# Full-row decay and rate products in preparation, attention's low parts on VectorE, and a later place for the first early operands

## The chip, the core and the metric

The kernel runs on one core of one Trainium2 chip. The metric is the device time of one execution in microseconds (us); the time before is the median of three executions. A profile is of one execution.

Engine names as in the profile: PE is TensorE (PEld its weight loads), DVE is VectorE, ACT is ScalarE, POOL is GpSimd, SP is SyncE, whose queue issues nearly all transfers between device memory and SBUF. "L514" is line 514 of the kernel.

## The reference

One layer of a hybrid encoder on 1024 tokens of width 1024, all in float32:

```
u = rmsnorm(h); cols = u @ w_in              # RWKV-7, HGRN2 and gate columns
rwkv7:  cols = cols + mu * (token_shift(cols) - cols)
        r, k, v, w_lo, a_lo, g_lo = split(cols)          # w_lo and a_lo: 64 columns each
        w_log = -softplus(-(w0 + tanh(w_lo) @ w2)) - 0.5  # decay
        a     = sigmoid(a0 + a_lo @ a2)                   # rate
        ... generalised delta-rule state over time, group norm, bonus, output gate
hgrn2:  ... gated linear recurrence in chunks of 64
h = h + (gate_a * y_a + gate_b * y_b) @ w_out
q, k, v = (rmsnorm(h) @ wq), (rmsnorm(mem) @ wk), (rmsnorm(mem) @ wv)   # 4 heads of 256, 256 memory tokens
h = h + softmax(q k / 16) v @ wo
h = h + (silu(u @ w1) * (u @ w3)) @ w2       # u = rmsnorm(h)
out = rmsnorm(h)
```

## The kernel before

**Products in three parts.** TensorE multiplies in a rounded float32 form. To keep the accuracy, an operand x is split: the high part is x rounded (a copy, on ACT, L282), the low part is x minus the high part (a subtraction, L286, on POOL or on DVE as `lo_eng` says). A product is then three matmuls into one PSUM tile (`mm3`, L300 to L302): high x high, high x low, low x high, 128 rows by 128 columns of weights against 512 or 256 columns. In the profile whi, wh, ah are high parts and wlo, wl, al low parts; whT and wlT are the parts of the first early operands of the feed-forward block.

**Stages.** Preparation (`rw_prep`, up to about 400 us) takes the RWKV columns in eight column blocks j of 128 and two halves h of 512 tokens: projections (pproj, 24 matmuls each) shifted in time, and between them `factors(j, h)`, which makes the decay sg and the rate aa from the low-rank columns. These lie in two tiles lw and la: of lw rows 0 to 63 hold the high part of tanh(w_lo) and rows 64 to 127 its low part; la the same for a_lo, with the halves exchanged. `LR` lists for each its tile, the rows of the high part (`own`) and those of the low part (`other`). The weight w2h holds the high part of w2 (or a2) twice, in both halves of the rows, so one matmul over 128 rows adds high x high and low x high. The third part, the low part of the weight (w2l) against the high part of the column, is a matmul over the 64 rows `own` alone (L514). Both write the PSUM tile pza. `tile_inputs(j)` makes w2h and w2l (L482, POOL); their pool has two buffers.

Mixing (to about 1298 us) has an order written out by the kernel's own planner; the change does not touch it. Then comes `attention_block`: values and keys (pvv, pk) from `mem`, the split of the mixed output y (`yraw`), the output product with w_out (`add_project`, PSUM tile pw), queries, scores, softmax and attended values for both token halves, and `add_project` with wo for each half. Beside the two kinds of output product run `w2_sums` (sums and differences of blocks of ffn_w2, stored for later) and, in the second half with wo, `early_blocks`: transposes (L1813), high and low parts (L1816 to L1819, L1820) of the feed-forward input of the first token half. Its PSUM tiles and those of the output product share eight buffers.

After it the feed-forward block works on half-size blocks with fewer products (seven for eight). Its first operands are made early: `weights(f, True)` loads the weights for f = 0 and 1, and `early_operands` makes from them differences on DVE (L2078, L2081, L2082) and splits them (whT, wlT; ACT and POOL) for the first products P5 and P4. The raw weights have ten buffers.

**What sets the order.** Outside mixing, a list scheduler fills each engine's queue: of the instructions that its simulation finds ready it takes the one earliest in the program; `high_priority(n)` counts a block's instructions as n places earlier. The queues then run in that order on the chip, each waiting for its own first instruction. The loads of the early weights are ordered on SP behind the last loads of wo (`behind`).

Of the kernel before, what the change touches and what calls it, by code (L numbers as in the profile page):

```python
# [18 lines left out]
P = 128  # L19
# [165 lines left out]
def tile_trunk(ctx, tc, x, mem, norm_mix_g, w_in, rw_mu, rw_w0, rw_w2, rw_a0, rw_a2, rw_g2,  # L185
# [93 lines left out]
    def split(hi, lo, src, hi_eng="act", lo_eng="pool"):  # L279

        if hi_eng == "act":
            nc.scalar.activation(hi, src, AF.Copy)  # L282
        else:
            nc.vector.tensor_copy(hi, src)
        e = nc.gpsimd if lo_eng == "pool" else nc.vector
        e.tensor_tensor(lo, src, hi.bitcast(F32), op=ALU.subtract)  # L286
# [136 lines left out]
    def rw_prep(rctx):  # L423
# [49 lines left out]
        def tile_inputs(j):  # L473
            w2r = fp.tile([P, 2, P], F32, tag="w2r", name="w2r", bufs=1)
            for n, w2 in enumerate((rw_w2, rw_a2)):
                for b in (0, 64):
                    nc.sync.dma_start(out=w2r[b:b + 64, n, :], in_=w2[0, :, j * P:(j + 1) * P])
            w2h = fp.tile([P, 2, P], F32R, tag="w2h", name="w2h")
            w2l = fp.tile([P, P], F32R, tag="w2l", name="w2l")
            nc.scalar.activation(w2h, w2r, AF.Copy)  # L480
            for n, (_, own, _) in enumerate(LR):
                nc.gpsimd.tensor_tensor(w2l[own, :], w2r[own, n, :], w2h[own, n, :].bitcast(F32), op=ALU.subtract)  # L482
            carry = fp.tile([P, 3], F32, tag="carry", name="carry")
            lnb = fp.tile([P, P], F32, tag="lnb", name="lnb")
            nc.sync.dma_start(out=lnb, in_=rw_ln_b[0, j * P:(j + 1) * P].partition_broadcast(P))
            krv = [[fp.tile([P, HALF], F32, tag=n, name=n, bufs=4) for h in range(NHALF)] for n in "krv"]
            tiles[j] = krv, w2h, w2l, lnb
            for n, mui in enumerate((8 + j, j, 16 + j)):
                if j == n == 0:
                    ahead.append(load_w(cols.pop(0)))  # L490
                    yield
                w = ahead.pop(0) if j == n == 0 else column()
                for h in range(NHALF):
                    if h and j == n == 0:
                        ahead.append(load_w(cols.pop(0)))
                    shifted(krv[n][h], w, mui, h, carry[:, n:n + 1])
                    yield
# [3 lines left out]
        def factors(j, h):  # L501
# [6 lines left out]

            sg, aa = T("sg"), T("aa")
            for n, (dst, bias) in enumerate(((sg, "w0"), (aa, "a0"))):  # L510
                t, own, _ = LR[n]
                ps = pz.tile([P, HALF], F32, tag="z", name="pza")
                nc.tensor.matmul(ps, w2h[:, n, :], t[:, sl], start=True, stop=False)
                nc.tensor.matmul(ps, w2l[own, :], t[own, sl], start=False, stop=True)  # L514
                nc.scalar.activation(dst, ps, AF.Sigmoid, bias=vc(bias, j))
            cum = T("cum")
            nc.vector.tensor_tensor_scan(cum, rst64, sg, 0.0, op0=ALU.mult, op1=ALU.add)
# [1130 lines left out]
    def attention_block(xctx):  # L1648
# [16 lines left out]
                nc.sync.dma_start(out=raw, in_=s3[:, k:k + 2, :])  # L1665
                yield k, raw

        def load_w(src, col, lo_eng=None):

            w = []  # L1670
            for k, raw in load_raw(src, col):
                hi, lo = (wp.tile([P, 2, W], F32R, tag=n, name=n) for n in ("whi", "wlo"))
                split(hi, lo, raw, lo_eng=lo_eng or ("pool", "dve")[k // 2 % 2])
                w += [(hi[:, n, :], lo[:, n, :]) for n in range(2)]
            return w

# [10 lines left out]
        def values(c):  # L1687
            cs = slice(c * HALF, (c + 1) * HALF)
            ps = [pp.tile([P, HALF], F32, tag="p", name="pvv") for _ in range(NMT)]
            for k in range(KT):  # L1690
                raw = w0.pop(0) if w0 else value_raw(c, k)
                hi, lo = (wp.tile([P, HALF], F32R, tag=n, name=n) for n in ("whi", "wlo"))
                split(hi, lo, raw, lo_eng=("pool", "dve")[k % 2])
                for t in range(NMT):
                    mm3(ps[t], *(m[:, k // 4, k % 4, t * P:(t + 1) * P] for m in mT), hi, lo, k == 0, k == KT - 1)
            for t in range(NMT):
                nc.scalar.activation(Vh[:, t, cs], ps[t], AF.Copy)
                nc.vector.tensor_tensor(Vl[:, t, cs], ps[t], Vh[:, t, cs].bitcast(F32), op=ALU.subtract)
# [23 lines left out]
        def w2_sums(fs, steps):  # L1722


            def load(f, y):
                for r in range(2):
                    rows = slice((f + r * HF) * P, (f + r * HF + 1) * P)
                    nc.sync.dma_start(out=y[:, 2 * r:2 * r + 2, :].rearrange("p c t -> p (c t)"), in_=ffn_w2[0, rows, :])

            def sums(f, y):  # L1730
                y11, y12, y21, y22 = (y[:, n, :] for n in range(4))
                nc.vector.tensor_tensor(y11, y12, y11, op=ALU.subtract)
                nc.gpsimd.tensor_tensor(y12, y22, y12, op=ALU.subtract)
                nc.gpsimd.tensor_tensor(y22, y22, y11, op=ALU.subtract)
                nc.vector.tensor_tensor(y21, y22, y21, op=ALU.subtract)
                nc.sync.dma_start(out=wsd[f], in_=y)

            loaded = []
            for loads, summed in steps:
                for place in loads:  # L1740
                    y, f = place(), next(fs)
                    load(f, y)
                    loaded.append((f, y))
                for _ in range(summed):
                    sums(*loaded.pop(0))
                yield
# [8 lines left out]
        def add_project(a, w, src, halves, ss=None, beside=iter(()), dst=None, between=lambda hs: None):  # L1755
# [15 lines left out]
            def split_next():  # L1771
                ck = todo[len(ww)]
                ww[ck] = [wp.tile([P, HALF], F32R, tag=n, name=n) for n in ("whi", "wlo")]
                split(*ww[ck], raws[len(ww) - 1], lo_eng=("pool", "dve")[ck[1] % 2])

            for c in range(NHALF):
                cs = slice(c * HALF, (c + 1) * HALF)
# [27 lines left out]
        def early_blocks(hs, hi, lo):  # L1805

            b12s, s1s = (vp.tile([P, HK, HALF], F32, tag=t, name="sums") for t in ("Vh", "Vl"))
            for k in range(HK):
                pts = []
                for kk in (k, k + HK):  # L1810
                    pts.append(pp.tile([P, HALF], F32, tag="p", name="pt"))
                    for i in range(4):
                        nc.tensor.transpose(pts[-1][:, i * P:(i + 1) * P], hs[i][:, kk * P:(kk + 1) * P], ident)  # L1813
                b12, s1 = b12s[:, k, :], s1s[:, k, :]
                h, l, g = hi[:, k, :], lo[:, k, :], vc("ffn", k + HK)
                nc.scalar.activation(b12, pts[0], AF.Copy, scale=vc("ffn", k))  # L1816
                nc.scalar.activation(h, pts[1], AF.Copy, scale=g)
                nc.vector.scalar_tensor_tensor(s1, pts[1], g, b12, op0=ALU.mult, op1=ALU.add)
                nc.vector.scalar_tensor_tensor(l, pts[1], g, h.bitcast(F32), op0=ALU.mult, op1=ALU.subtract)  # L1819
                split(hi[:, k + HK, :], lo[:, k + HK, :], s1)  # L1820
                nc.sync.dma_start(out=early_d[0, k], in_=b12)
                nc.sync.dma_start(out=early_d[1, k], in_=s1)
                yield
# [3 lines left out]
        for h, a in enumerate(yT):  # L1827
            for k in range(KT):
                raw = hp.tile([P, HALF], F32, tag="h", name="yraw")
                nc.sync.dma_start(out=raw, in_=yd[k, h])  # L1830
                split(a[0][:, k, :], a[1][:, k, :], raw, lo_eng="pool" if k % 2 else "dve")

        w2f = iter(range(HF))
        pairs = {}
# [230 lines left out]
    def weights(f, early=False):  # L2065

        if not early:
            return [[raw(w, k, (f + e) * P, HK, P) for e in (0, HF) for k in (0, HK)] for w in WS]
        A = [{}, {}]
        for b in (0, 2, 3, 1):  # L2070
            for n, w in enumerate(WS):
                A[n][b] = raw(w, b % 2 * HK, (f + b // 2 * HF) * P, HK, P, order=loads[min(f, 1)])
        return [[a[b] for b in range(4)] for a in A]

    def early_operands(A):
        T1, T4 = [], []
        for a11, a12, a21, a22 in A:
            tt(a21, a21, a11, op=ALU.subtract)  # L2078
            T1.append(operand(a21, "T1"))
        for a11, a12, a21, a22 in A:  # L2080
            tt(a22, a21, a22, op=ALU.subtract)  # L2081
            tt(a12, a22, a12, op=ALU.add)  # L2082
            T4.append(operand(a12, "T4"))
        return T1, T4
# [52 lines left out]

    with tc.high_priority(300):
        early = [weights(f, True) for f in range(2)]
        early = [early_operands(A) for A in early]  # L2140
    late = late_blocks()
    next(late)

    n = 0
# [181 lines left out]
```

## Time and profile before

| | |
|---|---|
| median of three executions | 2332.89 us (2332.19 to 2334.03) |
| the profiled execution | 2333.25 us, its span 2331.5 us |
| busy: PE, PEld | 2287.6 us (98%), 1863.8 us (80%) |
| busy: DVE, ACT, POOL | 1529.4 us (66%), 1136.0 us (49%), 1156.5 us (50%) |
| TensorE clock granted over the span | 0.995 |

Busy time of PE, DVE and POOL by stage, from the profile's stretches:

| stretch | us | PE | DVE | POOL | granted clock | DMA share |
|---|---|---|---|---|---|---|
| start, 0 to 100 | 100 | 84.05 | 64.10 | 43.26 | 0.97 | 0.49 |
| preparation, 100 to 380 | 280 | 280.00 | 223.70 | 141.28 | 1.00 | 0.45 |
| its end, 380 to 460 | 80 | 76.65 | 38.22 | 51.15 | 0.98 | 0.48 |
| mixing, 460 to 1298 | 838 | 832.34 | 581.89 | 488.06 | 1.00 | 0.38 |
| attention, 1298 to 1690 | 392 | 380.63 | 208.17 | 140.20 | 0.98 to 1.00 | 0.28 to 0.89 |
| feed-forward, 1690 to the end | 641.5 | 633.92 | 413.33 | 292.58 | 1.00 | 0.45 |

A row is read so: PE's busy time is the union of its matmuls' times, and a matmul counts as busy while it waits inside the pipeline, so the distance between the starts of two matmuls tells more than its duration. A share of a whole run is an average over stages with different limits; what counts is what PE waits for in a stage.

### The profile page before, as it was taken

Reading aid. Unit: us, or ns where it says so; the run is one execution under the profiler, and the core shown is the slowest. Engines: PE = TensorE matmul, PEld = TensorE weight load, DVE = VectorE, ACT = ScalarE, POOL = GpSimd, SP = SyncE. Lnnn points to the kernel's source line nnn. Section 1 sums busy time; section 2 is a strip of 40 time slices with the busy share of each in tenths; the row PEclk is TensorE's granted clock in tenths of the full one; section 3 lists DMA queues with packets and bytes.
Section 4 is the critical chain, followed back from the end, with each engine's and each line's share of the span. In section 5 each row is a group of like instructions: output and inputs, shape, how many; then the busy total and the mean of one; then the engine's idle time right before and its main releaser. Section 6 shows DMA issues by size and latency. Waiting matters only on the chain.

```text
span 2331.5 us, 47063 instructions
## 1 busy us (share of the span) xinstructions
PE 2287.6 (98%) x18262; PEld 1863.8 (80%) x18262; DVE 1529.4 (66%) x2425; ACT 1136.0 (49%) x2259; POOL 1156.5 (50%) x1201
## 2 busy tenths in 40 slices
PE   7999999999999999999999999999999999999998
PEld 5777777777888887888788778888788888888887
DVE  5787875576877767777666454544768675656655
ACT  6545455555565655654566323543453333334433
POOL 3555545655565655666566553113466555552212
PEclk9999999999999999999999999999999999999999
DMA  5344454332344343434334797215943323248653
GB/s 173 112 133 113 117 140 138 104 99 73 91 109 119 78 118 106 137 86 111 89 91 125 262 335 279 69 55 217 297 145 119 123 94 122 86 160 301 212 168 122
DMA packets 393691, 327.94 MB, mean 141 GB/s; under 512 B 107595, under 2 KB 318653, under 8 KB 392061
## 3 DMA queue, kind: packets, MB, share of 16 engines
q1 hardware_dynamic: 391549, 319.17, 44.9%
q0 software_dynamic: 1344, 4.72, 0.5%
q8 instruction: 144, 2.36, 0.4%
q10 hardware_dynamic: 576, 1.05, 0.1%
q14 instruction: 78, 0.64, 0.1%
HBM read 228.12 MB, written 96.21 MB: 139 GB/s over the span
## 4 chain that ended last, share of the span: by engine, by line
PE 76%; DVE 3%; DMA 2%; POOL 1%; issue 1%; ACT 1%; SPq 0%; POOLq 0%; ACTq 0%; DVEq 0%
PE pproj L103 21%; PE P L301 6%; PE P L302 6%; PE P L300 6%; PE acc L301 3%; PE acc L302 3%; PE acc L300 3%; PE cm L103 2%; PE pw L302 2%; PE pw L300 2%; PE pw L301 2%; PE psA L103 2%; PE psc L103 1%; PE po L103 1%; PE pq L302 1%; PE pq L301 1%
## 5 line engine op out<-in xcount | busy, mean ns | idle before, releaser
L103 PE MATMUL pproj<-uh,whi 128*128 128x512 f32 x768 | 319.9, 417 | 1.0 <-DVE q L103 1.0
L103 PE MATMUL pproj<-uh,wlo 128*128 128x512 f32 x768 | 301.0, 392 | 2.9 <-POOL wlo L103 2.3
L103 PE MATMUL pproj<-ul,whi 128*128 128x512 f32 x768 | 301.4, 392 | 0.0
L286 POOL TENSOR_TENSOR wlo<-wraw,whi 128x512 fp32r<-128x512 f32 (+1 forms) x86 | 117.0, 1362 | 224.5 <-ACT whi L282 210.0
L286 POOL TENSOR_TENSOR wl<-wraw,wh 128x512 fp32r<-128x512 f32 x87 | 121.4, 1403 | 204.4 <-ACT wh L282 160.8
L103 POOL TENSOR_TENSOR wlo<-wraw,whi 128x512 fp32r<-128x512 f32 x96 | 129.4, 1359 | 119.2 <-ACT whi L103 111.9
L282 ACT ACTIVATE whi<-wraw 128x512 fp32r<-128x512 f32 (+1 forms) x166 | 101.0, 617 | 174.5 <-PE pw L302 65.9
L300 PE MATMUL pproj<-uh,whi 128*128 128x512 f32 (+1 forms) x432 | 180.2, 417 | 1.1 <-ACT uh L328 0.7
L302 PE MATMUL pproj<-uh,wlo 128*128 128x512 f32 (+1 forms) x432 | 170.5, 395 | 1.9 <-POOL wlo L286 1.9
L103 PEld LDWEIGHTS pproj<-uh,whi 128*128 128x128 f32 x768 | 144.4, 188 | 34.3 <-DVE q L103 2.2
L103 PEld LDWEIGHTS pproj<-ul,whi 128*128 128x128 f32 x768 | 144.4, 188 | 32.4
L301 PE MATMUL pproj<-ul,whi 128*128 128x512 f32 (+1 forms) x432 | 170.2, 394 | 0.0
L103 PEld LDWEIGHTS pproj<-uh,wlo 128*128 128x128 f32 x768 | 144.9, 189 | 28.1 <-POOL wlo L103 2.7
L286 POOL TENSOR_TENSOR wlT<-wraw,whT 128x512 fp32r<-128x512 f32 x72 | 101.4, 1418 | 70.1 <-ACT whT L282 58.8
L282 ACT ACTIVATE wh<-wraw 128x512 fp32r<-128x512 f32 x143 | 87.2, 623 | 94.5 <-PE P L301 71.4
L103 ACT ACT_TABLE_LOAD x90 | 115.5, 1283 | 13.5 <-DVE m L103 6.4
L301 PE MATMUL acc<-wl,th 128*128 128x512 f32 x308 | 119.9, 389 | 0.0
L300 PE MATMUL acc<-wh,th 128*128 128x512 f32 x308 | 119.8, 389 | 0.0
L302 PE MATMUL acc<-wh,tl 128*128 128x512 f32 x308 | 119.8, 389 | 0.0
L300 PEld LDWEIGHTS pproj<-uh,whi 128*128 128x128 f32 (+1 forms) x432 | 81.5, 189 | 26.5 <-issue 6.7
L2270 DVE TENSOR_TENSOR tl<-tl,th 128x512 fp32r<-128x512 f32 x77 | 60.4, 797 | 62.6 <-ACT th L2269 62.3
L302 PE MATMUL pw<-whi,al 128*128 128x512 f32 x256 | 100.9, 394 | 0.3 <-DVE al L286 0.3
(457 smaller groups left out, 6386.2 us busy)
## 6 DMA issues: line engine op xcount, KB each, us to landing
wraw<-in_w_in_dram SPq DMA_DIRECT2D x148, 256.0 KB
wraw<-in_ffn_w_dram SPq DMA_DIRECT2D x145, 256.0 KB
y<-in_ffn_w_dram SPq DMA_DIRECT2D x22, 512.0 KB
wsum_d<-y SPq DMA_DIRECT2D x11, 1024.0 KB
hsum_d<-s SPq DMA_DIRECT2D x44, 256.0 KB
tl<-hsum_d SPq DMA_DIRECT2D x44, 256.0 KB
wraw<-wsum_d SPq DMA_DIRECT2D x44, 256.0 KB
hid_d<-s SPq DMA_DIRECT2D x33, 256.0 KB
```

The lines of the kernel that those rows point to most:

```text
L103: r = getattr(self.engine, op)(*a, **kw)
L282: nc.scalar.activation(hi, src, AF.Copy)
L286: e.tensor_tensor(lo, src, hi.bitcast(F32), op=ALU.subtract)
L300: nc.tensor.matmul(ps, ah, bh, start=first, stop=False)
L301: nc.tensor.matmul(ps, ah, bl, start=False, stop=False)
L302: nc.tensor.matmul(ps, al, bh, start=False, stop=last)
L2270: tt(hl, hl.bitcast(F32), hh.bitcast(F32), op=ALU.subtract)
```

## The change

1. Preparation: w2l becomes two tiles side by side of 128 rows each, one for the decay and one for the rate. The half of the rows that is not `own` is filled with zeros on POOL, and the matmul goes over all 128 rows of w2l and of lw or la. So the four products of a group have one form.
2. Attention: the low parts of the weights (values, keys, queries, w_out, wo) and of y, which alternated between POOL and DVE, and those of the early blocks' sums, which were POOL's, are all made on DVE. Two of the four subtractions of `w2_sums` go from POOL to DVE.
3. The early operands for f = 0 and 1 are made under `high_priority(150)` in place of 300; their loads stay at 300.

```
@@ tile_inputs
-            w2l = fp.tile([P, P], F32R, tag="w2l", name="w2l")
+            w2l = fp.tile([P, 2, P], F32R, tag="w2l", name="w2l")
             nc.scalar.activation(w2h, w2r, AF.Copy)
-            for n, (_, own, _) in enumerate(LR):
-                nc.gpsimd.tensor_tensor(w2l[own, :], w2r[own, n, :], w2h[own, n, :].bitcast(F32), op=ALU.subtract)
+            for n, (_, own, other) in enumerate(LR):
+                nc.gpsimd.memset(w2l[other, n, :].bitcast(F32), 0.0)
+                nc.gpsimd.tensor_tensor(w2l[own, n, :], w2r[own, n, :], w2h[own, n, :].bitcast(F32), op=ALU.subtract)
@@ factors
                 nc.tensor.matmul(ps, w2h[:, n, :], t[:, sl], start=True, stop=False)
-                nc.tensor.matmul(ps, w2l[own, :], t[own, sl], start=False, stop=True)
+                nc.tensor.matmul(ps, w2l[:, n, :], t[:, sl], start=False, stop=True)
@@ load_w of attention
-                split(hi, lo, raw, lo_eng=lo_eng or ("pool", "dve")[k // 2 % 2])
+                split(hi, lo, raw, lo_eng="dve")
@@ values
-                split(hi, lo, raw, lo_eng=("pool", "dve")[k % 2])
+                split(hi, lo, raw, lo_eng="dve")
@@ w2_sums
-                nc.gpsimd.tensor_tensor(y12, y22, y12, op=ALU.subtract)
-                nc.gpsimd.tensor_tensor(y22, y22, y11, op=ALU.subtract)
+                nc.vector.tensor_tensor(y12, y22, y12, op=ALU.subtract)
+                nc.vector.tensor_tensor(y22, y22, y11, op=ALU.subtract)
@@ split_next of add_project
-                split(*ww[ck], raws[len(ww) - 1], lo_eng=("pool", "dve")[ck[1] % 2])
+                split(*ww[ck], raws[len(ww) - 1], lo_eng="dve")
@@ early_blocks
-                split(hi[:, k + HK, :], lo[:, k + HK, :], s1)
+                split(hi[:, k + HK, :], lo[:, k + HK, :], s1, lo_eng="dve")
@@ the split of y
-                split(a[0][:, k, :], a[1][:, k, :], raw, lo_eng="pool" if k % 2 else "dve")
+                split(a[0][:, k, :], a[1][:, k, :], raw, lo_eng="dve")
@@ before the feed-forward block
     with tc.high_priority(300):
         early = [weights(f, True) for f in range(2)]
+    with tc.high_priority(150):
         early = [early_operands(A) for A in early]
```

More of the change, by code (lines that the diff above doesn't have):

```diff
@@ L510, in factors @@
             for n, (dst, bias) in enumerate(((sg, "w0"), (aa, "a0"))):
-                t, own, _ = LR[n]
+                t = LR[n][0]
                 ps = pz.tile([P, HALF], F32, tag="z", name="pza")
                 nc.tensor.matmul(ps, w2h[:, n, :], t[:, sl], start=True, stop=False)
-                nc.tensor.matmul(ps, w2l[own, :], t[own, sl], start=False, stop=True)
+                nc.tensor.matmul(ps, w2l[:, n, :], t[:, sl], start=False, stop=True)
                 nc.scalar.activation(dst, ps, AF.Sigmoid, bias=vc(bias, j))
@@ L1666, in load_raw, with load_w @@
                 yield k, raw
-        def load_w(src, col, lo_eng=None):
+        def load_w(src, col):
             w = []
```

## The prediction

> **What bounds the kernel now.** I read the page's busy times first, then busy time by stage, then what TensorE waits for, and last the order of time at the places that the change touches.
>
> ```profile
> span 2331.5 us, 47063 instructions
> PE 2287.6 (98%) x18262; PEld 1863.8 (80%) x18262; DVE 1529.4 (66%) x2425; ACT 1136.0 (49%) x2259; POOL 1156.5 (50%) x1201
> ```
>
> TensorE is busy for 98% of the span, but a matmul that waits inside its own pipeline counts as busy. So a gain can come from two places: from the idle 44 us, or from matmuls that start further apart than they need to.
>
> ```profile
> 100.00:380.00 280.00, 280.00 (x1240) 219.38 (x1239) 223.70 (x246) 136.62 (x200) 141.28 (x195) 1.00 0.45 120
> ...
> 1298.00:1440.00 142.00, 135.19 (x670) 114.10 (x669) 69.34 (x82) 47.31 (x84) 74.32 (x55) 0.98 0.89 317
> 1440.00:1600.00 160.00, 159.47 (x855) 136.44 (x854) 84.15 (x165) 80.01 (x173) 24.67 (x20) 1.00 0.28 93
> 1600.00:1690.00 90.00, 85.97 (x385) 70.28 (x384) 54.68 (x66) 35.14 (x66) 41.21 (x30) 0.98 0.88 290
> ```
>
> The columns are stretch, length, busy time of PE, PEld, DVE, ACT and POOL, granted clock, DMA share, GB/s. In preparation (100 to 380) TensorE never idles: every nanosecond between two matmul starts there is time of the kernel. In attention it idles for 142.0 - 135.2 = 6.8, 0.5 and 4.0 us, 11.4 in all. The waits of that stage say at what:
>
> ```profile
> PE pt L1813 <- DVE al L1819: 4.0, 1, 4.0
> PE pk L302 <- POOL wlo L286: 2.8, 1, 2.8
> PE pvv L301 <- POOL wlo L286: 1.7, 2, 0.9
> ```
>
> These three hold 8.5 of the 11.4 us, and all are waits for a low part on POOL or for DVE's queue, which is what the change moves.
>
> **Part A, preparation.** The order of time on PE around one group of decay and rate products (start, duration):
>
> ```profile
> 151.29 0.39 PE L513 MATMUL pza<-lw,w2h 128*128 128x512 f32 x1
> 151.61 0.49 PE L514 MATMUL pza<-lw,w2l 64*128 64x512 f32 x1
> 152.03 0.50 PE L513 MATMUL pza<-la,w2h 128*128 128x512 f32 x1
> 152.46 0.50 PE L514 MATMUL pza<-la,w2l 64*128 64x512 f32 x1
> 152.89 0.50 PE L300 MATMUL pproj<-uh,whi 128*128 128x512 f32 x1
> 153.22 0.40 PE L301 MATMUL pproj<-ul,whi 128*128 128x512 f32 x1
> 153.46 0.40 PE L302 MATMUL pproj<-uh,wlo 128*128 128x512 f32 x1
> ```
>
> Two neighbours of one form start 0.24 us apart (153.22 to 153.46). Where the form goes from 128 rows to 64 or back, the starts lie 0.32, 0.42, 0.43, 0.43 and 0.33 apart: five stretched steps, 153.22 - 151.29 = 1.93 us. With all four products on 128 rows they would be five plain steps, 5 x 0.235 = 1.18. Gain 0.75 us. Every second group stands behind transposes instead:
>
> ```profile
> 178.24 0.47 PE L513 MATMUL pza<-lw,w2h 128*128 128x512 f32 x1
> ...
> 180.26 0.40 PE L301 MATMUL pproj<-ul,whi 128*128 128x512 f32 x1
> ```
>
> Its five steps take 180.26 - 178.24 = 2.02 us. Five plain ones would take 1.18 (gain 0.84); if the first, behind the transposes, stays as long as a stretched one, 0.43 + 4 x 0.235 = 1.37 (gain 0.65). I take 0.75 here too, the middle. How often:
>
> ```profile
> L514 PE MATMUL pza<-lw,w2l x16: 492/492/502, 57.8 to 354.6; 64*128 64x512 f32 x16
> ```
>
> 16 groups x 0.75 = 12.0 us. The first two or three start before 100 us, where PE has other waits that may swallow it; I take 14 in full and two by half, 11.3 us. The cover: DVE is the next busiest, 223.7 of 280 us. Were PE to need only 280 - 13 x 0.75 = 270, DVE would stand at 83%, still not the bound, and ACT and POOL at about half. Bounds: 9 us gained (if the first and the last of the eight column blocks run into DVE) and 12.7 (8 x 0.75 + 8 x 0.84).
>
> What is added: 16 fills of a 64x128 half on POOL, in front of the subtraction in each block's input step.
>
> ```profile
> 416.83 0.21 POOL L103 MEMSET BP<- 128x128 f32 x1
> ```
>
> 16 x 0.21 = 3.4 us at most, beside 139 idle us of POOL in that stretch; the first use of the tile (57.8) comes long after it is made, so it costs nothing. The fill waits for the tile's slot, which was last read by the products two column blocks back, so it holds up nothing that is queued behind it on POOL. If POOL were full it would cost those 3.4 us.
>
> A rule that speaks against this part, with the row first:
>
> ```profile
> L300 PEld LDWEIGHTS pproj<-uh,whi 128*128 128x128 f32 x416 | 79.0, 190 | 25.5 <-issue 6.7 <-ACT uh L328 1.6 <-DVE BK L549 1.5
> ```
>
> A 128-row weight load takes 0.19 us, and yet the products start 0.24 apart with 512 columns each: the load is hidden behind the matmul before it. The Trainium skill, "TensorE: Matmul & The Clock Gate", Part 3, under what overlaps, says that a weight load overlaps with matmuls in flight only when its row group differs; by that, full-row loads would stand open and part A would bring about nothing. The trace does not bear it out for these loads.
>
> **Part B, attention's low parts, and its start.** 54 weight splits, 8 operand splits, 4 of the early blocks and 22 sums go from POOL to DVE.
>
> ```profile
> L286 POOL TENSOR_TENSOR wlo<-wraw,whi 128x512 fp32r<-128x512 f32 x54 | 74.5, 1381 | 194.9 <-ACT whi L282 180.5 <-PE pk L301 6.3 <-DMA wraw<-in_ffn_w_dram 3.8
> ```
>
> ```profile
> L286 DVE TENSOR_TENSOR wlo<-wraw,whi 128x512 fp32r<-128x512 f32 x54 | 48.7, 905 | 48.9 <-ACT whi L282 45.6 <-PE pt L322 2.0 <-DMA wraw<-in_xa_wk_dram 1.1
> ...
> L1912 DVE TENSOR_TENSOR al<-po,ah 128x512 fp32r<-128x512 f32 x16 | 11.1, 692 | 7.9 <-ACT ah L1911 7.9
> ```
>
> POOL takes 1.38 us for a weight's low part. DVE takes 0.69 for the same subtraction with one input in PSUM (last row), and 0.91 on average for the weights' low parts, whose two inputs lie in SBUF, while POOL works beside it. So 88 x 0.69 = 61 us come to DVE, and at least 54 x 0.21 = 11 of slowing go: DVE would have at most 208 + 50 = 258 of 392 us in the three stretches. It is not the bound on average; single places decide. The costliest, on PE, POOL and ACT:
>
> ```profile
> 1346.32 0.28 PE L301 MATMUL pk<-mT,whi 128*128 128x256 f32 x1
> 1349.43 0.58 PE L302 MATMUL pk<-mT,wlo 128*128 128x256 f32 x1 [2.84 <-POOL wlo L286]
> ...
> 1355.10 0.40 PE L300 MATMUL pw<-whi,ah 128*128 128x512 f32 x1
> ```
>
> ```profile
> 1347.67 1.71 POOL L286 TENSOR_TENSOR wlo<-wraw,whi 128x512 fp32r<-128x512 f32 x1
> ```
>
> ```profile
> 1343.52 1.14 ACT L282 ACTIVATE whi<-wraw 128x512 fp32r<-128x512 f32 x2
> ...
> 1352.43 0.63 ACT L282 ACTIVATE whi<-wraw 128x512 fp32r<-128x512 f32 x1 [6.82 <-DMA wraw<-in_w_out_dram]
> ```
>
> The high part is there at 1344.7 and the low part only at 1349.4, behind other low parts on POOL. ACT makes a high part in 0.57 us and DVE alone a low part in 0.69, so DVE stays close behind ACT and ends near 1346, about when PE asks. The wait (2.84) goes, and with it the slower clock behind it (0.98 granted in this stretch is 2.8 us of full speed lost; I put 1.3 of it here, the rest behind the value waits). What is late next: the first output weights, whose split waits for their load until 1352.4; that load stands in SP's queue behind the loads of yraw, which wait for slots that the same low parts free, so it comes earlier too, by 2 us or so. At the least PE starts the output product at 1352.4 + 0.63 + 0.69 = 1353.7 instead of 1355.1, a gain of 1.4; at the most the whole 4.1 and 0.9 us of the value waits (two of 0.9 at most, of which a load hides one). I take 3.2, nearer the upper end, since all that was late hangs on the low parts.
>
> **Part C, the end of attention.** The early loads keep their priority of 300; the first operands that are made of them get 150.
>
> ```profile
> 1660.76 2.80 DVE L2081 TENSOR_TENSOR wraw<-wraw 128x512 f32<-128x512 f32 x2
> 1663.49 1.75 DVE L2082 TENSOR_TENSOR wraw<-wraw 128x512 f32<-128x512 f32 x1
> 1665.16 0.74 DVE L1819 SCALAR_TENSOR_TENSOR al<-pt,VC,ah 128x512 fp32r<-128x512 f32 x1
> ```
>
> ```profile
> 1666.04 0.63 PE L1813 MATMUL pt<-ident,tok 128*128 128x128 f32 x4 [4.03 <-DVE al L1819]
> ```
>
> Three subtractions of the early operands stand in DVE's queue ahead of the low part that frees the PSUM tile, for 1665.16 - 1660.76 = 4.4 us; beside POOL two of them take 2.80. The clock granted in this stretch, 0.98 of 90 us, is 1.8 us lost, most of it behind this wait: 4.0 + 1.4 = 5.4 in all. With 150 these subtractions rank behind that low part, so the wait should mostly go. On the other side DVE gets eight low parts more in this stretch (5.5 us) and loses about as much slowing, and it is full here; the operands for the first P5 product are needed only after the last output products. I take 4.5, bounds 5.4 gained and 4 lost (one chain of subtraction, high part on ACT and POOL's 1.4 before the first product, with the slow clock).
>
> **The rest.** The 22 sums and the output and query weights: in their stretch (1440 to 1600) PE idles for 0.5 us in all. More in DVE's queue beside the softmax can cost from -0.5 to 1.4 us (two low parts); I take 0.5 lost, the middle.
>
> Sum: -11.3 - 3.2 - 4.5 + 0.5 = -18.5. The profiled execution took 2333.25 us (span 2331.5), 0.36 above the median of 2332.89. 2333.25 - 18.5 - 0.36 = 2314.4.
>
> **Rivals.** (1) The waits of attention stay or move: the order on DVE comes out with another operand in front, or PE then waits for the output weights. For it: DVE's full queue around 1660. Then A, 1.4 from B and up to 4 lost: 2333 - 11.3 - 1.4 + 0 to 4 = 2320 to 2324. (2) Preparation does not return its time. Either each full-row load stands open behind the product before it: the steps stay at 0.24 + 0.19 = 0.43, as long as now, and the time is 2333 - 7.2 = 2326. Against it are the 0.24 us steps of all other full-row products; chance 0.03. (That is the skill's rule of Part 3 above.) Or DVE takes over as the bound of preparation, against which stands its 83%; a third of A left gives 2322; chance 0.07. (3) Slower: operands with 150 free their weight slots later; SP's queue is in order, so the next loads of the feed-forward weights block the h_d stores and the hn loads behind them, and TensorE waits for the late blocks. For it: ten slots serve 24 early loads. Against it: the first late block is needed only after six products of 12 matmuls, 6 x 12 x 0.235 = 17 us. A wait of 14.5 us eats all that A and B bring, and from 19 on the kernel is slower by 0.2%. If all 16 low parts of the early operands, 16 x 1.38 = 22 us on POOL, came in front of those loads, it would be 2333 - 14.5 + 22 = 2341.
>
> **How the numbers follow.** The forecast 0.62; rival 1 0.23; rival 2 0.10 in both forms; rival 3 0.05. The forecast's own range is 2310 (12.7 + 5.0 + 5.4) to 2319. Eight in ten: 2309 to 2323. A measurement tells about 0.2%, 4.7 us, from no change: faster needs less than 2328.2, which the forecast, rival 1 and nearly all of rival 2 give: faster 0.91; same 0.05; slower 0.04.
>
> **What would show it.** A: no 64-row pza, steps of 0.24, a block of preparation 1.5 us shorter than now. B: no wait at pk, an earlier pw. C: no 4 us wait at L1813 and a granted clock of 1.00 there. Wrong would be: blocks of preparation of the old length, new waits for DVE near 1340 to 1360 or 1680 to 1700, or a wait for hn.

## The result and the profile after

| | before | changed | ratio, 95% interval |
|---|---|---|---|
| median | 2333.46 us (2332.19 to 2334.96, 4 runs) | 2309.59 us (2308.82 to 2316.52, 4 runs) | 0.9904, 0.9884 to 0.9924 |
| the profiled execution, its span | 2333.25, 2331.5 us | 2309.72, 2308.0 us | |

The kernel is 23.9 us faster; 18.5 was forecast. The time lies 0.4 us below the forecast's own range of 2310 to 2319 and at the fast edge of the eight-in-ten range of 2309 to 2323. In a later comparison the changed kernel gave 0.9900 (0.9885 to 0.9915).

The busy times on the page of the changed kernel:

```profile
PE 2270.0 (98%) x18262; PEld 1860.1 (81%) x18262; DVE 1558.0 (68%) x2513; ACT 1134.2 (49%) x2259; POOL 1037.3 (45%) x1129
```

PE is still at 98%. DVE has 88 instructions more and 28.6 us more work, POOL 119.2 us less. Where the time went is read from stretches between the same products in both traces. Those of the changed kernel (stretch, length, busy time of PE, PEld, DVE, ACT, POOL, granted clock, DMA share, GB/s):

```profile
93.12:379.15 286.03, 285.57 (x1311) 231.98 (x1310) 229.87 (x254) 146.80 (x217) 154.00 (x217) 0.99 0.48 126
...
1291.98:1334.72 42.74, 41.12 (x242) 34.93 (x240) 27.36 (x46) 24.38 (x45) 1.57 (x3) 1.00 0.97 328
...
1567.09:1663.15 96.06, 96.06 (x439) 78.29 (x437) 65.33 (x99) 40.19 (x79) 12.02 (x8) 1.00 0.88 286
1663.15:1711.38 48.23, 47.31 (x221) 38.44 (x220) 29.77 (x42) 29.20 (x52) 32.24 (x24) 1.00 0.56 182
```

Three of the same stretches in the kernel before:

```profile
95.56:393.12 297.56, 297.02 (x1311) 231.12 (x1310) 229.48 (x254) 147.28 (x217) 152.85 (x207) 0.99 0.45 121
...
1305.30:1355.10 49.80, 43.60 (x243) 37.66 (x241) 27.72 (x30) 26.59 (x48) 30.70 (x24) 0.93 0.89 296
...
1586.34:1688.09 101.75, 97.72 (x438) 79.61 (x437) 59.37 (x76) 40.40 (x79) 42.86 (x31) 0.98 0.83 278
```

All stretches side by side:

| from, to | before | changed | difference |
|---|---|---|---|
| start, third group of decay and rate products | 95.56 us | 93.12 us | -2.44 |
| third group, end of preparation's products | 297.56 (clock 0.99) | 286.03 (0.99) | -11.53 |
| to the first product of mixing | 80.22 | 80.07 | -0.15 |
| mixing, to the first pvv | 831.96 | 832.76 | +0.80 |
| first pvv, first pw | 49.80 (clock 0.93) | 42.74 (1.00) | -7.06 |
| first pw, first transposes of the softmax | 114.57 | 115.70 | +1.13 |
| to the second pw | 116.67 | 116.67 | 0.00 |
| wo, to the first P | 101.75 (clock 0.98) | 96.06 (1.00) | -5.69 |
| first P products | 46.91 | 48.23 | +1.32 |
| the rest | 596.50 | 596.62 | +0.12 |
| sum | | | -23.50 |

So there are three gains, where the three parts were made, and two places that gave 2.4 us back. What PE waited for from 1285 to 1750 us of the changed kernel:

```profile
PE pw L300 <- ACT whi L282: 0.7, 1, 0.7
PE pvv L301 <- DVE wlo L286: 0.7, 3, 0.2
PE P L300 <- ACT hB L2021: 0.6, 1, 0.6
...
PE pw L300 <- ACT ah L282: 0.4, 1, 0.4
```

The 4.0 of the transposes, the 2.8 of pk and the 1.7 of pvv for POOL are gone. The new rows are those of pw and of P; pvv now waits 0.7 us for DVE.

### The profile page after: what moved, and what is told of

It is laid out like the page before. It is cut to its first block, busy times and chain, and to the rows that moved or that the text cites. A ratio compares the mean times of both kernels' runs of the same rounds, so it can differ in the third digit from the quotient of the medians.

```text
span 2308.0 us, 47067 instructions
## 1 busy us (share of the span) xinstructions
PE 2270.0 (98%) x18262; PEld 1860.1 (81%) x18262; DVE 1558.0 (68%) x2513; ACT 1134.2 (49%) x2259; POOL 1037.3 (45%) x1129
## 4 chain that ended last, share of the span: by engine, by line
PE 73%; DVE 4%; DMA 3%; POOL 2%; issue 1%; ACT 1%; SPq 0%; POOLq 0%; ACTq 0%; DVEq 0%
PE pproj L103 21%; PE P L301 6%; PE P L302 6%; PE P L300 6%; PE acc L301 3%; PE acc L302 3%; PE acc L300 3%; PE pw L302 3%; PE pw L301 2%; PE pw L300 2%; PE cm L103 2%; PE psA L103 2%; PE psc L103 1%; PE po L103 1%; PE pq L301 1%
## 5 line engine op out<-in xcount | busy, mean ns | idle before, releaser
L277 POOL TENSOR_TENSOR ss<-ss,nhalf 128x4 f32<-128x4 f32 (+1 forms) x7 | 6.2, 881 | 323.1 <-DMA wraw<-in_xa_wo_dram 186.6
L286 DVE TENSOR_TENSOR wlo<-wraw,whi 128x512 fp32r<-128x512 f32 x134 | 93.1, 701 | 55.3 <-ACT whi L282 53.4
L300 PE MATMUL pw<-whi,ah 128*128 128x512 f32 x256 | 100.6, 393 | 1.2 <-ACT whi L282 0.7
```

The source lines that it names most:

```text
L277: nc.gpsimd.tensor_tensor(dst, tmp, nhalf[:, 0:n], op=ALU.pow)
L300: nc.tensor.matmul(ps, ah, bh, start=first, stop=False)
```

## The experiments

The differences below are of medians within one comparison, or of landmarks (starts of the same PE product) in the traces. The landmarks scatter a little: the four kernels that leave preparation as it was start its third group 0.2 to 1.6 us and its fifth 0.2 to 3.1 us sooner than the profiled execution before, keep most of that distance to the end of preparation's products, and then lose 0.3 to 1.1 us on it in mixing. Differences of that size at those places are not read as effects; the mean over the later groups is not touched by them. One part of it may belong to the change: from 57 to 66 us the granted clock is 0.81 (1.7 us lost) in five of the seven traces with a 64-row product (not in e4 and e9), and 1.00 in all seven with full rows. No run decides whether the 64-row products bring it about.

| kernel | median, us | before beside it | ratio, 95% interval |
|---|---|---|---|
| e1_prep_only | 2320.53 | 2332.93 | 0.9949, 0.9937 to 0.9962 |
| e2_low_only | 2326.89 | 2332.93 | 0.9978, 0.9969 to 0.9986 |
| e3_prio_only | 2332.53 | 2332.93 | 0.9997, 0.9988 to 1.0007 |
| e4_no_prep | 2322.18 | 2332.93 | 0.9956, 0.9943 to 0.9969 |
| e5_decay_full | 2318.28 | 2331.13 | 0.9941, 0.9929 to 0.9954 |
| e6_half_rows_together | 2316.93 | 2331.13 | 0.9938, 0.9925 to 0.9952 |
| e7_late_first | 2309.50 | 2331.13 | 0.9907, 0.9893 to 0.9920 |
| e9_prio_late_first | 2327.51 | 2331.13 | 0.9981, 0.9972 to 0.9989 |
| e8_y_alternates | 2310.67 | 2331.84 | 0.9906, 0.9892 to 0.9921 |
| e10_wout_first | 2310.89 | 2331.84 | 0.9905, 0.9890 to 0.9920 |
| e11_both | 2306.96 | 2331.84 | 0.9889, 0.9872 to 0.9905 |
| e12_changed_again | 2309.96 | 2331.84 | 0.9900, 0.9885 to 0.9915 |

### The three parts one by one

**Preparation alone** (the kernel before with the first two hunks of the change).

> The kernel before with the change's first part alone: both low products of preparation on all 128 rows, attention as before. If the steps to and from a 64-row product are what cost (0.42 us against 0.23), each of the 16 groups starts its next product some 0.8 us sooner, preparation ends 13 to 14 us sooner, and this is all kept to the end: 2319 to 2321 us by the median before of 2333.46. If preparation's gain only looks like that because attention's part covers for it (the value weights arriving later than the rows of attention then need them), attention's first waits grow by what preparation returned and the time stays at 2324 us or more. The rest of attention, with the 3.1 us wait of pk and the 4.3 us wait at the hand-over, should be where it was.

2320.53 us, 12.4 less than before. Preparation's products end 13.3 us sooner by the trace, and the kernel's end 13.8. The waits of attention are there as before:

```profile
PE pt L1814 <- DVE al L1820: 3.9, 1, 3.9
PE pk L302 <- POOL wlo L286: 2.8, 1, 2.8
```

So preparation's time is kept, and attention does not live on it: the first theory.

**Low parts alone** (the hunks of attention, `early_operands` still at 300).

> The kernel before with the second part alone: attention's low parts and sums on VectorE, the early operands at their old priority, preparation as before. If POOL's low parts were what the 3.1 us wait of pk and the waits of pvv stood on, attention is 6 to 8 us shorter up to the query stage; the 4.3 us wait at the hand-over should stay if its cause is where the early operands stand in their queues, and go if its cause is POOL's work. First case: 2326 to 2328 us; second: 2321 to 2324 us. If VectorE's own low parts are late instead, pk's wait turns into waits of pvv and pw and the time stays at 2331 to 2334 us.

2326.89 us, 6.0 less (0.22%). The 2.8 us wait of pk is gone, the hand-over's stays nearly whole, and pw waits instead, here for its weights and then 0.8 us for ah:

```profile
PE pt L1813 <- DVE al L1819: 3.7, 1, 3.7
PE pw L300 <- ACT whi L282: 1.0, 1, 1.0
```

By landmarks this kernel gains 8.1 us from the first pvv to pk's last product, and 5.3 are left at the softmax's first transposes. The hand-over is therefore not POOL's doing: with all low parts on DVE it waits 3.7 of 4.0 us.

**The priority alone.**

> The kernel before with the third part alone: the early operands behind their loads at priority 150, everything else as before. If the place in the queue is what the 4.3 us wait at the hand-over stands on, the wait goes and the time is 4 to 6 us less: 2327 to 2330 us. If it needs the low parts on VectorE too (POOL making the low half of the second operand, behind its other low parts), the wait stays or shrinks by a part only and the time is 2331 to 2334 us. The first 1650 us should be those of the kernel before.

Neither theory: the wait at the hand-over is gone (5.6 us from there to the first P), and yet the time is the same, 2332.53 against 2332.93. The first P products give 5.0 us back. PE at that place, and DVE before it:

```profile
1720.44 0.39 PE L302 MATMUL P<-hB,wl 128*128 128x512 f32 x1
1723.72 0.49 PE L300 MATMUL P<-hB,wh 128*128 128x512 f32 x1 [2.90 <-ACT hB L2019]
1724.51 0.79 PE L301 MATMUL P<-lB,wh 128*128 128x512 f32 x1 [0.29 <-DVE lB L2020]
1725.10 0.63 PE L302 MATMUL P<-hB,wl 128*128 128x512 f32 x1
1725.53 0.63 PE L300 MATMUL P<-hB,wh 128*128 128x512 f32 x1
```

```profile
1703.36 1.23 DVE L2110 TENSOR_TENSOR T<-wraw 128x512 f32<-128x512 f32 x1 [4.82 <-DMA wraw<-in_ffn_w_dram]
1704.52 0.68 DVE L2112 TENSOR_TENSOR wraw<-T,wraw 128x512 f32<-128x512 f32 x1
1705.12 1.40 DVE L2020 SCALAR_TENSOR_TENSOR lB<-pth,VC,hB 128x512 fp32r<-128x512 f32 x2
```

A sum T of `products` waits 4.82 us at the head of DVE's queue for its load. The late blocks' lB stands behind it, then their fS, whose high parts on ACT stand ahead of the next hB, for which P waits 2.90. The products after that wait start 0.43 apart instead of 0.23. In the kernel before, the same sum comes 1705.88 - 1688.09 = 17.8 us after the first P:

```profile
1705.88 1.52 DVE L2110 TENSOR_TENSOR T<-wraw 128x512 f32<-128x512 f32 x1 [3.21 <-DMA wraw<-in_ffn_w_dram]
```

In e3 it comes 1703.36 - 1681.62 = 21.7 us after it. PE reached its first P 6.5 us sooner and the load came only 2.5 us sooner: the wait at the hand-over had covered this one. In e3 SP issues that load behind those of hn and of the early blocks, where it waits for their transfers; its record there shows no wait for a free slot.

**Low parts and priority, preparation as before.**

> The changed kernel with preparation put back: attention's low parts on VectorE and the early operands behind their loads. If the parts add up, this gives what the change gives without preparation's 13 to 14 us: 2322 to 2324 us. If the three parts overlap (one cover serving two), it is either nearer to the changed kernel (2316 us or less) or nearer to the kernel before (2327 us or more). In the traces the attention start's gain is 8 us up to pk's last product and 6 us after the waits of pw that follow; I expect the same here.

2322.18 us, 10.75 less. With e1 the ratios add up: 0.51% + 0.44% = 0.95%, against 0.96% for the whole change. Parts B and C alone give 0.22% and 0.03%, together 0.44%. That is more than their sum, by about as much as the intervals allow, so I do not build on it; the trace does not decide it, since its execution (2326.39 us) was the longest of the five.

### What a 64-row product costs

> The changed kernel, but the rate's low product on its own 64 rows again, the decay's on all 128. If each step between a 128-row and a 64-row product costs 0.2 us, two of the four such steps of a group are back: the groups' starts fall behind those of the changed kernel by 0.41 us each, preparation ends 6.5 to 7 us later, and the time is 2316 to 2317 us against 2309.6. If instead it is the change of the row group between the decay's rows and the rate's that costs, one 64-row product alone costs little and the time stays at 2310 to 2312 us.

```
+                rs = slice(0, P) if n == 0 else LR[n][1]
-                nc.tensor.matmul(ps, w2l[:, n, :], t[:, sl], start=False, stop=True)
+                nc.tensor.matmul(ps, w2l[rs, n, :], t[rs, sl], start=False, stop=True)
```

A group in the changed kernel, and the same in e5 (start, duration):

```profile
146.46 0.39 PE L515 MATMUL pza<-lw,w2h 128*128 128x512 f32 x1
146.69 0.39 PE L516 MATMUL pza<-lw,w2l 128*128 128x512 f32 x1
146.92 0.40 PE L515 MATMUL pza<-la,w2h 128*128 128x512 f32 x1
147.15 0.40 PE L516 MATMUL pza<-la,w2l 128*128 128x512 f32 x1
147.39 0.39 PE L300 MATMUL pproj<-uh,whi 128*128 128x512 f32 x1
147.62 0.39 PE L301 MATMUL pproj<-ul,whi 128*128 128x512 f32 x1
```

```profile
149.42 0.39 PE L515 MATMUL pza<-lw,w2h 128*128 128x512 f32 x1
...
149.88 0.40 PE L515 MATMUL pza<-la,w2h 128*128 128x512 f32 x1
150.21 0.49 PE L517 MATMUL pza<-la,w2l 64*128 64x512 f32 x1
150.63 0.50 PE L300 MATMUL pproj<-uh,whi 128*128 128x512 f32 x1
150.96 0.40 PE L301 MATMUL pproj<-ul,whi 128*128 128x512 f32 x1
```

The five steps take 1.16 us in the changed kernel and 1.54 with one 64-row product: 0.33 into it, 0.42 out of it, and 0.33 once more. One excursion to 64 rows thus costs 0.38 us; two cost 1.93 - 1.16 = 0.77 in the kernel before. By landmarks the groups fall behind by 0.41 us each, half of preparation's 0.82, as the first theory says; the time, 2318.28, is 1.3 us above what I expected from it.

> The changed kernel with both low products of a group on their own 64 rows, as before, but in the order high, high, low, low: the same work as before the change, with two steps between 128 and 64 rows instead of four, and one step from one half of the rows to the other. If the step between row counts is what costs, preparation is 0.41 us a group slower than in the changed kernel (2316 to 2317 us). If the half-row products themselves are the slow ones, it is 0.82 a group (2322 to 2323 us); if every change of rows costs alike, three steps are left and it is 0.6 a group (2319 to 2320 us).

```
+            pzs = [pz.tile([P, HALF], F32, tag="z", name="pza") for _ in range(2)]
+            for n in range(2):
+                nc.tensor.matmul(pzs[n], w2h[:, n, :], LR[n][0][:, sl], start=True, stop=False)
+            for n in range(2):
+                own = LR[n][1]
+                nc.tensor.matmul(pzs[n], w2l[own, n, :], LR[n][0][own, sl], start=False, stop=True)
...
-                nc.tensor.matmul(ps, w2h[:, n, :], t[:, sl], start=True, stop=False)
-                nc.tensor.matmul(ps, w2l[:, n, :], t[:, sl], start=False, stop=True)
```

```profile
150.10 0.39 PE L514 MATMUL pza<-lw,w2h 128*128 128x512 f32 x1
150.33 0.40 PE L514 MATMUL pza<-la,w2h 128*128 128x512 f32 x1
150.66 0.50 PE L517 MATMUL pza<-lw,w2l 64*128 64x512 f32 x1
150.66 0.50 PE L517 MATMUL pza<-la,w2l 64*128 64x512 f32 x1
151.09 0.50 PE L300 MATMUL pproj<-uh,whi 128*128 128x512 f32 x1
151.43 0.40 PE L301 MATMUL pproj<-ul,whi 128*128 128x512 f32 x1
```

The trace shows what none of the three theories had: the two 64-row products lie on opposite halves of the rows and start together. The five steps take 1.33 us, 0.17 more than with full rows: one excursion, 0.40, less one product's step, 0.23, which the pair saves. By landmarks a group is 0.21 slower, not 0.41. The median of 2316.93 is what 0.41 a group was to give, 7.4 us above that of the changed kernel with e7's edit, run beside it (2309.50); but 16 groups at 0.21 make only 3.4 of it, and the rest is open. The profiled execution, the longest of the five, starts its third group 3.1 us later than the changed kernel's and loses 3.0 instead of 1.3 us at the first P. In the groups, the row counts cost, not the half-row products, and three quarters of what the change took out (0.60 of 0.77 in these) can be had by order alone; the medians do not show that much of a gain. The Trainium skill, "TensorEngine Tiling (Array Packing)", Key Properties, says that a change of the tiling mode drains the engine and that tiles work independently; these rows agree with both, with 0.38 us an excursion and one start for two tiles.

### What is late next

**The first P products.** In the changed kernel they wait behind the same load as in e3:

```profile
1683.14 0.69 DVE L2112 TENSOR_TENSOR T<-wraw 128x512 f32<-128x512 f32 x1 [4.80 <-DMA wraw<-in_ffn_w_dram]
...
1684.35 1.40 DVE L2022 SCALAR_TENSOR_TENSOR lB<-pth,VC,hB 128x512 fp32r<-128x512 f32 x2
```

Two kernels put the late blocks ahead: e7 on top of the changed kernel, e9 on top of e3.

```
             if n > 5 and n % 2 == 0:
-                next(late)
+                with tc.high_priority(100):
+                    next(late)
```

> The kernel before with the early operands at priority 150 and the late blocks at priority 100. With the first of these alone, the hand-over's 5.6 us were given back at the first products (3.3 us wait for hB at 1720 us, and later ones). If they were given back because VectorE's lB and fS stand behind sums T that wait 4.8 us for a load, they are kept here: 2327 to 2329 us. If they were given back because the loads themselves (290 to 400 GB/s through this stage) are what the feed-forward waits for, the wait turns up at another place and the time stays at 2331 to 2334 us.

> The changed kernel, with the late blocks put at priority 100, so that VectorE's lB and fS stand ahead of the sums T and wraw of the first products, which wait for a load (4.8 us) in the changed kernel. If that load is what the late blocks and the first products P are behind, the two waits of P at 1702 us (1.0 and 0.8 us) go and the time is about 1.3 us less: 2308 to 2308.5 us. If the transposes or ScalarE's copies hold them as well, nothing changes: 2309 to 2310 us. If the sums T, now behind, come late for products P7 and P6, it gets slower: 2311 us or more.

e9 takes 2327.51 us, 3.6 less than the kernel before beside it, where e3 gained nothing. By landmarks e9 keeps 3.4 of the 5.4 us that it gains at the hand-over, e3 0.6 of 5.6: most of what the priority frees is kept once the late blocks do not stand behind that load. The edit moves their work on every engine, not on VectorE alone. The waits from 1600 to 1790 us are now

```profile
PE pth L2017 <- DVE hn L2001: 1.6, 1, 1.6
PE pt L1813 <- DVE al L1819: 0.3, 1, 0.3
```

so the next limit is the load of hn. e7 loses 0.3 us instead of 1.3 at the first P (the waits of 1.0 and 0.8 between starts there shrink to one of 0.6), but its median, 2309.50 (0.9907), cannot be told from the changed kernel's 2309.59 (0.9904): its trace, of the longest of its four executions, is 2.1 us behind the changed kernel's when it comes there (1.15 of it by the first pvv) and loses 0.9 in the last products. The mechanism is shown; a gain in time from it alone is not.

**The first products pw.** PE in the changed kernel, and ACT before it:

```profile
1333.69 0.28 PE L302 MATMUL pk<-mT,wlo 128*128 128x256 f32 x1
1334.72 0.50 PE L300 MATMUL pw<-whi,ah 128*128 128x512 f32 x1 [0.75 <-ACT whi L282]
...
1338.64 0.50 PE L300 MATMUL pw<-whi,ah 128*128 128x512 f32 x1 [0.41 <-ACT ah L282]
```

```profile
1334.04 0.63 ACT L282 ACTIVATE whi<-wraw 128x512 fp32r<-128x512 f32 x1 [4.94 <-DMA wraw<-in_w_out_dram]
```

ACT had waited 4.94 us for w_out, whose first load SP issues behind twelve loads of y.

> The changed kernel, with the first four loads of w_out issued ahead of the last eight of y, which nothing can use before pk's last product frees their place. In the changed kernel SP issues w_out's first load at 1329.4 us, ScalarE gets it at 1334.0, and the start of pw loses 2.2 us in four gaps (1.03, 0.73, 0.79 and 0.53 us between starts where 0.23 is the step). If the place in SP's queue is the cause, the gaps shrink to some 0.5 us in all and the time is about 1.7 us less: 2307.5 to 2308.5 us. If the transfers themselves are the limit (340 GB/s through this stage), y's loads come later by as much, the wait moves from w_out to ah, and the time stays at 2309 to 2310 us.

```
+                if h and not k:
+                    for n in range(4):
+                        first.append(rp.tile([P, HALF], F32, tag="wraw", name="wraw"))
+                        nc.sync.dma_start(out=first[-1], in_=w_out[0, n * P:(n + 1) * P, 0:HALF])
                 raw = hp.tile([P, HALF], F32, tag="h", name="yraw")
```

SP and PE of e10:

```profile
1320.72 3.67 SPq L1836 DMA_DIRECT2D wraw<-in_w_out_dram  x4
1324.43 4.80 SPq L1838 DMA_DIRECT2D yraw<-y_d  x8
```

```profile
1334.30 0.28 PE L302 MATMUL pk<-mT,wlo 128*128 128x256 f32 x1
1334.42 0.40 PE L300 MATMUL pw<-whi,ah 128*128 128x512 f32 x1
```

pw starts one step behind pk, all its gaps are gone, and y does not come late: the place in the queue was the cause. The trace keeps 2 us of it through the queries and ends 1.4 us sooner than the changed kernel's. The median does not show it: 2310.89 us in six runs from 2308.30 to 2314.90, against 2309.96.

> The changed kernel itself, unaltered, beside the two versions meant to better it: 2308.5 to 2310.5 us by the four runs of it so far (2308.82 to 2316.52, three of them within 2308.8 to 2309.8).

It gave 2309.96 (2307.11 to 2311.07, five runs), as expected.

> The changed kernel with w_out's first four loads ahead of the last eight of y, and the late blocks at priority 100. If both of the changed kernel's remaining waits go (2.2 us at the start of pw, 1.3 us at the first products P) and neither comes back elsewhere, 2306 to 2307 us; if the stage's transfers are the limit in both places, 2309 to 2310 us.

2306.96 us (2306.44 to 2307.79, four runs), 3.0 below the changed kernel beside it; its slowest run is faster than four of the five. The ratios' intervals overlap, so this is likely the better kernel, by 0.1%, not certainly. Of both waits little is left, and a part of the hand-over's is back:

```profile
PE pt L1816 <- DVE al L1822: 0.8, 1, 0.8
```

**The low parts of y.**

> The changed kernel with the low parts of y by turns on POOL and VectorE, as before the change, all the rest of the change kept. If y's low parts matter (they stand on VectorE between the low parts of the values' and the keys' weights, 0.69 us each alone and up to 1.7 beside POOL), the waits of pvv and of pw grow and the time is 2311 to 2313 us; if what matters is only that the weights' low parts left POOL, the time stays at 2309 to 2310 us, or is a little less, as VectorE has eight low parts fewer.

2310.67 us: inside the scatter of the changed kernel. pk waits 0.9 us again and pw starts 1.4 us after pk's last product, against 0.6 in e12; at the softmax's first transposes the trace is 1.1 us behind e12's. What matters is that the weights' low parts left POOL; y's are worth about 1 us.

## Why the prediction was right, and where its sizes were off

**Part A: forecast -11.3, measured about -13.** The mechanism is shown by e1, e5 and e6. The group at 146.46 takes 1.16 us against 1.93, a gain of 0.77; one behind transposes, forecast with the middle of two values, takes 1.24 against 2.02, a gain of 0.78. By landmarks the mean over the last 14 groups is 11.53 / 14 = 0.82, so a little more than the five steps was gained. Two steps of the working were careful: plain steps at 0.235, where they are 0.23, and half the gain for the first two groups, whose true worth cannot be told from the scatter of the start. By the traces the upper bound of 12.7 was too low, 16 x 0.82 = 13.1; the medians (12.4 less in e1) cannot tell the two apart. The cover held: DVE is at 229.87 of 286.03 us, 80% (forecast 83%). The rule on weight loads of the Trainium skill, "TensorE: Matmul & The Clock Gate", Part 3, by which this part would have brought nothing, is not borne out: the full-row products now start 0.23 us apart.

**Part B: forecast -3.2, bounds 1.4 to 5.0; measured -7.06 + 1.13 = -5.9, past the upper bound.** The mechanism is right; the term that was too small is the slow clock. The sum has 1.3 us of it behind pk's wait, and what the prediction put behind the value waits never came into it. The stretch from pvv to pw ran at 0.93 for 49.8 us, 3.4 us of full speed lost, and runs at 1.00 now. In the trace before, two pieces of 3.41 us at half speed make this up, 1.7 us lost in each, one among the value waits and one behind pk's:

```profile
1315.28:1318.69 3.41, 3.14 (x7) 2.48 (x8) 2.63 (x3) 2.59 (x5) 3.11 (x3) 0.50 1.05 366
1349.41:1352.82 3.41, 3.38 (x16) 3.39 (x17) 0.04 (x1) 0.39 (x1) 0.00 (x0) 0.50 0.90 276
```

All four traces with the old low parts have the second (before, e1, e3, e9), only two the first (before, e3): 1.7 of the 7.06 us may be scatter. And I had w_out come 2 us earlier; its high part starts 1334.04 - 1291.98 = 42.1 us after the first pvv instead of 1352.43 - 1305.30 = 47.1, 5.0 earlier, as I read it because every slot that DVE frees sooner lets SP issue sooner. That w_out would be late next was right, and e10 shows it. I also undersized what DVE wins by POOL's absence. The page's row for the weights' low parts:

```profile
L286 DVE TENSOR_TENSOR wlo<-wraw,whi 128x512 fp32r<-128x512 f32 x134 | 93.1, 701 | 55.3 <-ACT whi L282 53.4
```

All 54 that moved cost 26.5 us net: the row before for all stages was 66.6 us in 80. The 88 instructions added 28.6 us to DVE, where 88 x 0.69 = 61 less 11 had been reckoned: 32 us of slowing went, three times the forecast's, if all the difference is POOL's absence.

**Part C: forecast -4.5, bounds 5.4 gained to 4 lost; measured -5.69 at the hand-over, + 1.32 at the first P, -4.4.** The wait and its slow clock went whole (clock 0.98 to 1.00; 0.50 from 1666.86 to 1670.27 before, 1.7 us lost where 1.4 was reckoned), and the bound of 5.4 was passed by 0.3. That the net is near the forecast is luck: something was given back that the sum did not have, and its size changes from trace to trace, 1.3 here, 1.9 in e12, 4.5 in e4. It comes at the place that rival 3 named, the late blocks, but not by its mechanism: no wait for a slot on SP shows there, but a sum T on DVE that waits for its load, as e3 and e9 show. By itself this part is worth nothing (0.9997).

**The rest: forecast +0.5.** The queries lose nothing. Mixing is 0.80 longer, which the experiments' scatter covers. Rival 1 (waits that move) came true for 2.4 us of B's and C's 12.8; rivals 2 and 3 did not, though the wait for hn that was named as a sign of being wrong is there in e9 (1.6 us).

## What to carry to other kernels

A product on half of the rows among full-row ones paid 0.38 us on the way in and out here, so fill it up with zeros, or put two on opposite halves side by side. When a wait goes, look in each in-order queue for the instruction that stands on a load just behind it: here one VectorE sum took 5.0 us of a 5.6 us gain back until the work behind it went first. Price a wait of about 3 us on TensorE with the slow products after it (1.7 us behind each of three such waits here), and a POOL operation that leaves with what VectorE gains beside it.

## What the hardware showed that I had not expected

- Two 64-row matmuls on opposite halves of the rows start at the same time (150.66 and 150.66 in e6), and one excursion from 128 to 64 rows and back costs 0.38 us.
- After the 2.90 us wait in e3 the products start 0.43 us apart instead of 0.23, at half the clock for 3.41 us (the stretch 1724.16:1727.57 of e3, granted clock 0.50), as after the waits of 2.84 and 4.03 us in the kernel before. The longest single wait does not decide it: the piece at 1315.28 stands among waits of 0.9 and 1.4 us, while after a wait of 2.31 us in e6 (1713.35) the clock stayed at 1.00.
- VectorE's subtractions with both inputs in SBUF lost more to POOL than their mean told: 834 ns for 80 of them before, 701 for 134 after. The Trainium skill, "SBUF — State Buffer", SBUF: two separate sides, says that these two engines share a port pair, and that a VectorE instruction with two SBUF inputs and a GpSimd instruction that reads SBUF hold it by turns, each for its whole time while the other is blocked. A subtraction of 128x512 that takes 0.68 us while POOL is idle (1704.52 in e3) and 1.75 beside one of POOL's (1663.49 before, in the prediction) agrees with it.
